# Small tasks of a mixing stage placed behind chosen chunks of the next products, with a stated order, and the rotary tables moved into that stage

## The chip, the cores and the metric

The kernel runs on one core of a Trainium2 chip, as one program. The metric is the device time of one execution in microseconds (us). Besides the timed runs there is one profiled execution, whose trace records every instruction on the engines PE (matrix products), DVE (vector), ACT (scalar functions), POOL and on SP, which here issues most of the loads.

## The reference, cut to what matters

One decoder layer on 256 tokens of width 2048, in float32:

```
x1 = x + 1/2 * SwiGLU_1(RMSNorm(x))                 # "ffn1", d_ff = 5632
P  = RMSNorm(x1) @ w_in                             # one projection, cut into named pieces
     A: gated linear attention (GLA), 4 heads, per-token decay from a low-rank projection
     B: NSA, 8 query heads on 2 key/value heads: compressed + sliding-window branches, rotary, gates
     C: attention of 4 heads into 256 memory tokens (keys and values are mem @ wmem)
x2 = x1 + concat(A, B, C) @ w_out                   # A to C and this are the "mixing stage"
x3 = x2 + 1/2 * SwiGLU_2(RMSNorm(x2))               # "ffn2"
y  = RMSNorm(x3)
```

Rotary embedding turns queries and keys by angles position x inverse frequency; their sines and cosines are the "rotary tables".

## The kernel before, in words

**A product.** All 256 tokens are two blocks t of 128 rows, and the activations stay on chip. Each product runs over the weights in chunks: one load of 128x1024 values (two slices kk of 128 x 512; `chunk`, L299), issued by SP, into a buffer of the pool `raw`. `split` (L290, L291) makes of a chunk a rounded part h on ACT and the rest l = r - h on DVE. PE then multiplies three times for each (kk, t), h by the activations' h (L304), l by their h (L305), h by their l (L306; `mm3`): 12 matmuls of 128x512 a chunk, 8 chunks for a product of 512 columns (agq has 296 columns, and chunks of 128x592).

**Slabs.** The two feed-forward stages go by slabs of 512 hidden columns. A slab is computed either in a form with seven products of half size, or "plain". By count of the built program the first takes 174 product matmuls and the second 192. `ffn(..., plain=(1,))` makes slab 1 of ffn1 plain. Each slab begins by turning activations (transposes of `c` or `g`, L390), which marks its place in the trace.

**Small tasks.** Everything else is small: transposes, norms, softmaxes, decay factors, score products. The framework schedules them among the product's instructions for each engine, and puts in the semaphore waits. The engines then work through their orders without exchanging any. A pool's buffer is free again when the readers of what lay there are done. Pools of a new stage are laid over those of the stage before in the order in which the dictionaries `FFN_SB`, `MIX_SB` list them.

**Places that matter here.** `prepare` computes the rotary tables on DVE in steps during ffn1's slab 1: nine pieces, each L616, L610, L611, L612, L618 (see `frac` and the loop over `PIECES`), then the tables ckn, skn, cqn, sqn (L631 to L633). At the end of ffn1 `last_of_ffn1` turns the last 512 columns of the residual `acc` (L341) and finishes the sums of squares. The mixing stage runs the projections agq, gkks (then kc), gv, gr, kwvs, vw and the queries; after gkks the keys of the first set are normed and turned through the rotary tables (`ra`, L772 to L776) and transposed (L786). GLA's decay levels (L827, L849) and masked products stand between gkks and gv. `nsa_group(g, ...)` runs eight steps of scores (L1028 to L1030), softmax, transposes of the weights `e` (L1072) and their product with values (L1077); at the end of a block come L1103 and L1108. `mem_heads` norms the memory queries and keys and transposes them (L1131). wmem is multiplied (two products), memory attention (L1156) follows, then wout, whose evictions add to `acc` (L1203), and ffn2, whose first chunk again needs the last 512 columns turned (L341).

Of the kernel before, what the change touches and what calls it, by code (L numbers as in the profile page):

```python
# [188 lines left out]
def _body(tc, A):  # L189
# [10 lines left out]
    def stage(name, sb, ps):  # L200

        stages.close()
        P.clear()
        sizes.clear()
        for n, b in ps.items():
            P[n] = stages.enter_context(tc.tile_pool(name=name + n, bufs=b, space=PSUM, reuse_waits="tile"))
        for n, (b, size) in sb.items():
            P[n] = stages.enter_context(tc.tile_pool(name=name + n, bufs=b, reuse_waits="tile"))
            sizes[n] = size
# [74 lines left out]

    def split(r, parts=1):
        n = r.shape[1]
        h, l = hi(n), lo(n)
        for i in range(parts):
            sl = slice(i * n // parts, (i + 1) * n // parts)
            act.activation(h[:, sl], r[:, sl], AF.Copy)  # L290
            dve.tensor_sub(l[:, sl], r[:, sl], f(h[:, sl]))  # L291
        return h, l

# [9 lines left out]
    def mm3(out, ah, al, wh, wl, first, last):  # L303
        pe.matmul(out, ah, wh, start=first, stop=False)  # L304
        pe.matmul(out, ah, wl, start=False, stop=False)  # L305
        pe.matmul(out, al, wh, start=False, stop=last)  # L306

    def mmchunk(banks, ah, al, k0, w, first, last):
        h, l = w
        n = h.shape[2]  # L310
        for kk, t in ((0, 0), (1, 0), (0, 1), (1, 1)) if first else ((0, 0), (0, 1), (1, 0), (1, 1)):
            sl = slice(t * 128, t * 128 + 128)
            mm3(banks[t][:, :n], ah[:, k0 + kk, sl], al[:, k0 + kk, sl], h[:, kk], l[:, kk],
                first and kk == 0, last and kk == 1)
# [20 lines left out]
    def transposed(j, g, th, tl):  # L335
        for k in range(4):
            if k % 2 == 0:
                pt = tbank().rearrange("p (k t) -> p k t", k=2)
# [249 lines left out]
    def prepare():  # L588

        early = raw(N_EARLY)  # L590
        nc.sync.dma_start(early, A["early"])
        C.update({n: early[:, o:o + w] for n, (o, w) in EARLY.items()})
        nc.sync.dma_start(kept, A["kept"])
        posi = sbuf("raw", "posi", I32, 3)
        nc.sync.dma_start(posi, A["pos"])
        posf = small(3, "posf")
        dve.tensor_copy(posf, posi)
        rots = raw(), raw()
# [36 lines left out]


        dve.tensor_copy(identb, ident)
        for i in range(2):
            dve.tensor_copy(maskb[:, i], C["tri"])
        r = raw(1024)  # L640
        nc.sync.dma_start(r, A["lmask"])
        dve.tensor_copy(lmask.rearrange("p l t -> p (l t)"), r)
# [25 lines left out]
    def before1(at):  # L668
# [12 lines left out]
        elif at[0] == 1:  # L681
            next(prep, None)
        elif at == (3, 10):
            norm_mem()

    prep = prepare()
    ffn("ffn1", hh, hl, r1, after1, before1, plain=(1,))
    xh, xl = st1["h"], st1["l"]
    r2, rm, r2q, r2n = (keep.tile([128, 2], F32, name=n) for n in ("r2", "rm", "r2q", "r2n"))

    def last_of_ffn1(c):
        if c == 1:
            norm_and_turn1(3)
            dve.tensor_copy(r2, finish_ss(ss1))
            dve.tensor_copy(rm, finish_ss(ssm))
            dve.tensor_scalar_mul(r2q, r2, 0.125)
            dve.tensor_scalar_mul(r2n, r2, -1.0)
# [5 lines left out]

    def scaled(dst, src, s):
# [4 lines left out]
    own = stages.enter_context(tc.tile_pool(name="own", bufs=1))  # L709
# [4 lines left out]
    for dst, sl in ((lev.rearrange("p l t -> p (l t)"), slice(0, 1024)), (levb, slice(1024, 1152))):  # L714
        r = raw(sl.stop - sl.start)
        nc.sync.dma_start(r, A["lev"][:, sl])
        act.activation(dst, r, AF.Copy)
    b = proj("agq", last_of_ffn1)
    ga = own.tile([128, 2, 17], F32, name="ga")
    dve.memset(ga, 1.0)  # L720
    gates = own.tile([128, 2, 24], F32, name="gates")
# [10 lines left out]
    pt = tbank()  # L732
    for t in range(2):
        pe.transpose(pt[:17, t * 128:t * 128 + 128], ga[:, t], ident)
    act.activation(gaT[:17], pt[:17, :256], AF.Copy)
    la = []
    xs, ex = (t512(n).rearrange("p (t d) -> p t d", t=2) for n in ("xs", "ex"))
    for t in range(2):
        pa = mbank()[:, :256]
        pe.matmul(pa, gaT[:17, t * 128:t * 128 + 128], C["wab"][:17], start=True, stop=True)  # L740
        act.activation(xs[:, t], pa, AF.Copy)
    dve.scalar_tensor_tensor(ex, xs, -1.0, xs, op0=ALU.mult, op1=ALU.min)
    act.activation(ex, ex, AF.Exp)
    act.activation(ex, ex, AF.Ln, bias=1.0)
    dve.scalar_tensor_tensor(xs, xs, 0.0, ex, op0=ALU.min, op1=ALU.subtract)
    for t in range(2):
        lah, lal = part(lab, t, 256), lab[:, t * 512 + 256:t * 512 + 512]
        act.activation(lah, xs[:, t], AF.Copy)
        dve.tensor_sub(lal, xs[:, t], f(lah))
        la.append((lah, lal))  # L750

    b = proj("gkks")
# [65 lines left out]
    for t in range(2):  # L818
        pool.memset(at[t], 0.0)
        for hp in range(2):  # L820
            hsl = slice(hp * 128, hp * 128 + 128)
            tsl = slice(t * 128, t * 128 + 128)
            dec = part(sb, 3 + 2 * hp, 1024).rearrange("p (l t) -> p l t", l=8)
            for half in range(2):
                pb = mbank()
                tm = lev[:, 4 * half:4 * half + 4].rearrange("p l t -> p (l t)")
                pe.matmul(pb, la[t][0][:, hsl], tm, start=True, stop=False)  # L827
                pe.matmul(pb, la[t][1][:, hsl], tm, start=False, stop=t == 0 or half == 0)
                if t == 1 and half == 1:
                    pe.matmul(pb[:, 384:], la[t][0][:, hsl], levb, start=False, stop=False)  # L830
                    pe.matmul(pb[:, 384:], la[t][1][:, hsl], levb, start=False, stop=True)
                act.activation(dec[:, 4 * half:4 * half + 4], pb.rearrange("p (l t) -> p l t", l=4), AF.Exp)
            for pl, s in enumerate(SIZES):
                for odd in range(2):
                    dv = dec[:, pl].rearrange("p (b o s) -> p b o s", o=2, s=s)[:, :, odd]
                    sv = gT[:, 1 - odd, hp, tsl].rearrange("p (b o s) -> p b o s", o=2, s=s)[:, :, odd]
                    dve.tensor_tensor(dv, dv, sv, op=ALU.mult)
            dve.tensor_tensor(far[:, hp, t], dec[:, 7], gT[:, 1 - t, hp, tsl], op=ALU.mult)
            for i0 in range(0, 8, 4):
                pbs = [mbank().rearrange("p (l t) -> p l t", l=4) for h in range(2)]  # L840
                for li in range(4):
                    i = i0 + li
                    for h in range(2):
                        ps = slice(64 * h, 64 * h + 64)
                        if i == 7:
                            lhs, rhs = gT[ps, 1, hp, tsl], gT[ps, 0, hp, tsl]
                        else:
                            lhs = rhs = dec[ps, i]
                        pe.matmul(pbs[h][:, li], lhs, rhs, start=True, stop=True)  # L849
                for h in range(2):  # L850
                    for li in range(4):
                        dve.copy_predicated(at[t][:, 2 * hp + h], lmask[:, i0 + li], pbs[h][:, li])
    pbs = [mbank() for h in range(2)]
    for hp in range(2):
        for h in range(2):
            ps = slice(64 * h, 64 * h + 64)
            pe.matmul(pbs[h][:, hp * 128:hp * 128 + 128], far[ps, hp, 0], far[ps, hp, 1], start=True, stop=True)
    for h in range(2):
        act.activation(at[2].rearrange("p (a b) t -> p a b t", b=2)[:, :, h],
                       pbs[h][:, :256].rearrange("p (a t) -> p a t", a=2), AF.Copy)  # L860
# [66 lines left out]
    b = proj("gv", spread("k", 0))  # L927
# [5 lines left out]
    b = proj("gr", spread("k", 4))  # L933
# [12 lines left out]
    for t in range(2):  # L946
# [13 lines left out]
    oh, ol = t16("oh"), t16("ol")  # L960
# [6 lines left out]
    for t in range(2):  # L967
# [9 lines left out]
    b = proj("kwvs", spread("v", 0))  # L977
# [26 lines left out]
    def pipelined(n, scores, softmax, apply):  # L1004
        scores(0)
        softmax(0)
        for i in range(n):
# [3 lines left out]
            if i + 1 < n:  # L1011
                softmax(i + 1)

    def nsa_group(g, qT):
# [96 lines left out]
        pipelined(8, scores, softmax, apply)  # L1111
# [9 lines left out]
    def mem_heads(b, rr, g, dst):  # L1121
        for t in range(2):
# [6 lines left out]
            pt = tbank().rearrange("p (h t) -> p h t", h=4)  # L1129
            for h in range(4):  # L1130
                pe.transpose(pt[:, h], v3[:, h], ident)  # L1131
            act.activation(dst[:, :, t * 128:t * 128 + 128], pt, AF.Copy)

    b = proj("mq")
    mem_heads(b, r2, C["mqn"], mT[0])
    nsa_group(1, q1)
    for i in range(2):
        b = [bank(), bank()]
        for c in range(4):
# [6 lines left out]
            for e in range(2):  # L1146
                mmchunk(b, h, l, 2 * e, chunk(A["wmem"][i, 2 * c + e]), c == e == 0, c == 3 and e == 1)
        if i == 0:
            mT.append(b4("mT").rearrange("p (h t) -> p h t", h=4))
            mem_heads(b, rm, C["mkn"], mT[1])  # L1150
# [112 lines left out]
```

## Time and the profile before

| | |
|---|---|
| median of 3 runs | 1850.74 us (1849.97 to 1850.81) |
| the profiled execution's own time | 1849.49 us |
| its span in the trace | 1847.7 us |
| PE busy in the span | 1824.6 us (99%), 8483 matmuls |
| DVE busy | 1618.7 us (88%) |
| ACT busy | 1076.6 us (58%) |

The span runs from the first to the last recorded instruction; some 1.8 us of the execution's time lie around it. Busy time counts an engine's records and overlaps within a pipelined engine are merged. A matmul's record of 0.39 us is longer than the pitch from one to the next, since they are pipelined, so the pitch is what a matmul costs.

### The profile page before, as it was taken

What the parts mean: (1) busy time and instruction counts of PE and PEld (TensorE: products, weight loads), DVE (VectorE), ACT (ScalarE), POOL (GpSimd) and SP (SyncE); (2) the same over time, 40 slices, a digit from 0 to 9 for tenths busy, and PEclk for the clock granted to TensorE, in tenths of its full rate; (3) what the DMA queues carried; (4) which work ended last, traced back from release to release, by engine and by line L of the source; (5) the groups of instructions that cost most, each with busy time, mean ns of one, the idle gap of its engine ahead of it and who ended that gap; (6) DMA issues with size and microseconds to landing.
All of it is one profiled execution on the core that took longest, in us unless ns stands there. A gap on an engine that the chain in (4) does not pass through costs nothing.

```text
span 1847.7 us, 23758 instructions
## 1 busy us (share of the span) xinstructions
PE 1824.6 (99%) x8483; PEld 1486.1 (80%) x8483; DVE 1618.7 (88%) x2075; ACT 1076.6 (58%) x1366; POOL 81.1 (4%) x106
## 2 busy tenths in 40 slices
PE   8999999999999999999999999999999999999997
PEld 6888888888888888777877787888888888888886
DVE  8989999999999986667677854999999999999996
ACT  7455665566556557533457643656656565665564
POOL 0000000000000000001000000000000000000000
PEclk9999999999999999999999999999999999999999
DMA  9677877677767735555644554776778677766771
GB/s 347 232 231 239 297 213 219 230 246 218 228 229 234 222 134 198 167 183 169 231 147 137 171 183 147 260 254 198 234 232 255 197 224 240 253 206 217 239 236 72
DMA packets 111224, 395.78 MB, mean 214 GB/s; under 512 B 12544, under 2 KB 12800, under 8 KB 110976
## 3 DMA queue, kind: packets, MB, share of 16 engines
q1 hardware_dynamic: 102896, 364.36, 56.7%
q0 software_dynamic: 8208, 29.89, 9.2%
q8 instruction: 67, 1.10, 0.2%
q14 instruction: 53, 0.43, 0.1%
HBM read 392.10 MB, written 2.10 MB: 213 GB/s over the span
## 4 chain that ended last, share of the span: by engine, by line
PE 92%; DVE 4%; DMA 1%; ACT 1%; issue 1%; POOL 1%; SPq 0%; ACTq 0%; POOLq 0%; DVEq 0%
PE pm L305 21%; PE pm L304 21%; PE pm L306 21%; PE px L304 8%; PE px L306 8%; PE px L305 8%; PE pt L390 1%; DVE l L291 1%; DMA r<-ffn1g 1%; PE pm L884 1%; POOL y L328 0%; PE px L849 0%; PE pt L341 0%; DVE exg L940 0%; PE po L1077 0%
## 5 line engine op out<-in xcount | busy, mean ns | idle before, releaser
L290 ACT ACTIVATE h<-r 128x1024 fp32r<-128x1024 f32 (+2 forms) x829 | 869.9, 1052 | 641.0 <-PE pm L306 477.7
L291 DVE TENSOR_TENSOR l<-r,h 128x1024 fp32r<-128x1024 f32 (+2 forms) x829 | 981.2, 1207 | 128.1 <-ACT h L290 115.9
L304 PE MATMUL px<-h,gx 128*128 128x512 f32 x616 | 239.9, 389 | 0.0
L306 PE MATMUL px<-h,gx 128*128 128x512 f32 x616 | 239.9, 389 | 0.0
L305 PE MATMUL px<-l,gx 128*128 128x512 f32 x616 | 239.9, 389 | 0.0
L304 PE MATMUL pm<-h,sh 128*128 128x512 f32 x456 | 179.7, 394 | 0.0
L305 PE MATMUL pm<-l,sh 128*128 128x512 f32 x456 | 179.3, 393 | 0.0
L306 PE MATMUL pm<-h,sl 128*128 128x512 f32 x456 | 178.0, 390 | 0.0
L305 PE MATMUL pm<-l,hh 128*128 128x512 f32 x398 | 155.5, 391 | 2.6 <-DVE l L291 2.6
L304 PE MATMUL pm<-h,hh 128*128 128x512 f32 x398 | 154.2, 391 | 0.8 <-ACT h L290 0.8
L306 PE MATMUL pm<-h,hl 128*128 128x512 f32 x398 | 154.9, 390 | 0.0
L305 PE MATMUL pm<-l,zh 128*128 128x512 f32 x364 | 142.7, 392 | 0.3 <-DVE l L291 0.3
L306 PE MATMUL pm<-h,zl 128*128 128x512 f32 x364 | 142.6, 392 | 0.0
L304 PE MATMUL pm<-h,zh 128*128 128x512 f32 x364 | 142.1, 391 | 0.0
L304 PEld LDWEIGHTS px<-h,gx 128*128 128x128 f32 x616 | 115.7, 188 | 24.1 <-issue 0.2
L305 PEld LDWEIGHTS px<-l,gx 128*128 128x128 f32 x616 | 115.7, 188 | 23.9
L306 PEld LDWEIGHTS px<-h,gx 128*128 128x128 f32 x616 | 115.7, 188 | 23.9
L305 PE MATMUL pm<-l,xh 128*128 128x512 f32 (+2 forms) x320 | 120.2, 376 | 1.1 <-DVE l L291 1.0
L304 PE MATMUL pm<-h,xh 128*128 128x512 f32 (+2 forms) x320 | 121.3, 380 | 0.0
L306 PE MATMUL pm<-h,xl 128*128 128x512 f32 (+2 forms) x320 | 120.4, 377 | 0.0
L404 DVE SCALAR_TENSOR_TENSOR acc<-px,acc 128x512 f32<-128x512 f32 x154 | 105.6, 686 | 6.3 <-PE px L306 4.6
L306 PEld LDWEIGHTS pm<-h,sl 128*128 128x128 f32 x456 | 85.7, 188 | 17.5
(336 smaller groups left out, 2630.7 us busy)
## 6 DMA issues: line engine op xcount, KB each, us to landing
r<-ffn1u SPq DMA_DIRECT2D x88, 512.0 KB, 5.0
r<-ffn1d SPq DMA_DIRECT2D x88, 512.0 KB, 4.8
r<-ffn2u SPq DMA_DIRECT2D x88, 512.0 KB, 4.8
r<-ffn2d SPq DMA_DIRECT2D x88, 512.0 KB, 4.8
r<-ffn1g SPq DMA_DIRECT2D x87, 512.0 KB, 5.1
r<-ffn2g SPq DMA_DIRECT2D x87, 512.0 KB, 5.1
r<-wout SPq DMA_DIRECT2D x32, 512.0 KB, 3.3
r<-ffn2u POOLq DMA_DIRECT2D x30, 512.0 KB, 7.4
```

The source lines that it names most:

```text
L290: act.activation(h[:, sl], r[:, sl], AF.Copy)
L291: dve.tensor_sub(l[:, sl], r[:, sl], f(h[:, sl]))
L304: pe.matmul(out, ah, wh, start=first, stop=False)
L305: pe.matmul(out, ah, wl, start=False, stop=False)
L306: pe.matmul(out, al, wh, start=False, stop=last)
L390: pe.transpose(pt[:, k], g[:, k * 128:k * 128 + 128], ident)
L404: dve.scalar_tensor_tensor(a, pd, 0.5, a, op0=ALU.mult, op1=ALU.add)
L884: pe.matmul(pcs[n][32 * p:32 * p + 32], flats[n][:, c * 4 + p], r[:, p * 256:p * 256 + 256], start=c == 0, stop=c == 7, tile_position=(0, ...
```

## The change

Eight things change.

- `prepare` becomes `rotary`, a sequence of steps in the mixing stage: it makes one step at each chunk of agq and of gkks, and what is left follows gkks. Its table `early` (128x704) and `posi` are loaded into the mixing stage's pools `b4` and `ev`. Constants that `prepare` also loaded are made at one point of ffn1 (`constants`).
- ffn1 has no plain slab any more.
- The pools are listed in another order, so that in the mixing stage `b4` lies over ffn1's `hi`, and `wk`, `ev` and `own` over its `lo`, with `raw`, `hi` and `lo` behind them.
- At ffn1's end and at the end of the mixing stage the last transposes go in two parts behind the splits and products of chunks 1 and 2 of the next product, squares behind chunk 4, the sums behind chunk 5, and copies behind chunk 7.
- `behind_products` states that an instruction stands, on its engine, behind the last product instruction (or split) written so far.
- GLA's steps are called at chunks of gv and gr, and its output and its transposes at chunks of kwvs.
- The transposes of the memory heads come at the second half of the next memory product's first load.
- Memory attention goes by one step at each half chunk of the second memory product, and at chunks 1 to 5 of wout's first product.

```diff
-FFN_SB = {"raw": (11, 1024), "hi": (6, 1024), "lo": (6, 1024), "gx": (1, 2048), "wk": (5, 512)}
-MIX_SB = {"raw": (6, 1024), "hi": (5, 1024), "lo": (5, 1024), "b4": (6, 1024), "wk": (6, 512), "ev": (2, 512)}
+FFN_SB = {"hi": (6, 1024), "lo": (6, 1024), "raw": (11, 1024), "gx": (1, 2048), "wk": (5, 512)}
+MIX_SB = {"b4": (6, 1024), "wk": (6, 512), "ev": (2, 512), "own": None, "raw": (6, 1024), "hi": (5, 1024),
+          "lo": (5, 1024)}
...
-MIX_PS = {"pm": 3, "px": 2, "pt": 2, "po": 1}
+MIX_PS = {"px": 2, "pt": 2, "po": 1, "pm": 3}
...
+    def behind_products(*engines):
+
+        ex = ExitStack()
+        for i in [done[e] for e in engines or done]:
+            ex.enter_context(tc.issue_after(getattr(i, "ins", i)))
+        return ex
...
-    def prepare():
-
-        early = raw(N_EARLY)
+    def rotary():
+
+        early = b4("early")[:, :N_EARLY]
         nc.sync.dma_start(early, A["early"])
         C.update({n: early[:, o:o + w] for n, (o, w) in EARLY.items()})
-        nc.sync.dma_start(kept, A["kept"])
-        posi = sbuf("raw", "posi", I32, 3)
+        posi = sbuf("ev", "posi", I32, 3)
         nc.sync.dma_start(posi, A["pos"])
         posf = small(3, "posf")
+        yield
         dve.tensor_copy(posf, posi)
...
-    ffn("ffn1", hh, hl, r1, after1, before1, plain=(1,))
+    ffn("ffn1", hh, hl, r1, after1, before1)
...
+    def turn_last(c, ss, g, th, tl):
+
+        if c in (1, 2):
+            with behind_products():
+                transposed(3, g, th, tl, range(2 * c - 2, 2 * c))
+        if c == 4:
+            with behind_products():
+                square_acc(ss, 3)
...
+    rot = rotary()
+
+    def first_of_mix(c):
+        last_of_ffn1(c)
+        next(rot, None)
+        if c == 5:
+            load_levels()
...
-    b = proj("gkks")
+    b = proj("gkks", both(lambda c: next(rot, None), placed((1, turn_ga), (3, log_decay))))
+    for _ in rot:
+        pass
...
-    b = proj("gv", spread("k", 0))
+    lv, dc = (lambda i: lambda: levels(*divmod(i, 2))), (lambda i: lambda: decayed(*divmod(i, 2)))
+    b = proj("gv", both(spread("k", 0), placed((1, lv(0)), (3, lv(1)), (4, dc(0)), (5, lv(2)), (6, dc(1)),
+                                               (7, lv(3)))))
...
-    b = proj("gr", spread("k", 4))
+    b = proj("gr", both(spread("k", 4), placed((1, dc(2)), (3, dc(3)), (4, far_products))))
...
-    b = proj("kwvs", spread("v", 0))
+    b = proj("kwvs", both(spread("v", 0), placed((1, lambda: gla_out(0)), (2, lambda: gla_out(1)),
+                                                 (4, lambda: turn_out(0)), (5, lambda: turn_out(1)))))
...
+                if (c, e) == (1, 0):
+                    with behind_products("pe"):
+                        turn_mem()
                 mmchunk(b, h, l, 2 * e, chunk(A["wmem"][i, 2 * c + e]), c == e == 0, c == 3 and e == 1)
+                if i == 1 and c > 0:
+                    with behind_products("pe"):
+                        next(mem_attention, None)
...
     def before2(at):
-        if at == 1:
-            norm_and_turn2(3)
-            dve.tensor_copy(r3, finish_ss(ss2))
+        if at in range(8):
+            turn_last(at, ss2, C["g2"], zh, zl)
```

Three places in the engines' orders show what these lines do. First the queue of SP at the end of ffn1, where the last loads of ffn1 (ffn1d) are followed by the first loads of the mixing stage (win_agq); `[waits ...]` lists the semaphores by which a load is held. Before:

```order
L299 DMA r<-ffn1d 128x1024 [waits DMAHW6_49,DVE_49]
L716 DMA r<-lev 128x1024 [waits DMAHW2_49,DMAHW7_49,DVE_49,Activation_49]
L716 DMA r<-lev 128x128 [waits DMAHW6_49,DMAHW0_49,DVE_49]
L299 DMA r<-win_agq 128x592 [waits DMAHW4_49,DMAHW1_49]
L299 DMA r<-win_agq 128x592
L299 DMA r<-win_agq 128x592 [waits DMAHW3_49]
```

Of the change:

```order
L309 DMA r<-ffn1d 128x1024 [waits DMAHW4_49,DVE_49]
L611 DMA posi<-pos 128x3 [waits DMAHW5_49,DVE_49,PE_49]
L608 DMA early<-early 128x704 [waits DMAHW6_49,Activation_49]
L309 DMA r<-win_agq 128x592 [waits DMAHW7_49,DMAHW0_49]
L309 DMA r<-win_agq 128x592
L309 DMA r<-win_agq 128x592 [waits DMAHW1_49]
```

Two loads have moved ahead of all of agq, and the first of them waits for PE. The semaphore's value is that of the last matmul but one of ffn1, which reads the last buffer of ffn1's pool `lo`, over which `posi` is laid.

The second place is DVE at the same point: the last eviction of ffn1 into `acc` (L404 before, L414 in the change), then the splits of agq (l<-r,h 128x592; L291, now L294). Before:

```order
L404 SCALAR_TENSOR_TENSOR acc<-pm,acc 128x512
L291 TENSOR_TENSOR l<-r,h 128x592 x2
L333 SCALAR_TENSOR_TENSOR xl<-pt,gains,xh 128x256
L351 TENSOR_REDUCE s_6110<-ss_127 128x2
L291 TENSOR_TENSOR l<-r,h 128x592
```

Of the change:

```order
L414 SCALAR_TENSOR_TENSOR acc<-pm,acc 128x512
L625 MEMSET rot 128x192
L614 CAST posf<-posi 128x3
L616 CAST maskb<-early 128x128 x2
L621 TENSOR_TENSOR rot<-early,posf 128x192
L623 CAST rot<-rot 128x192
L624 TENSOR_TENSOR rot<-rot 128x192
L635 TENSOR_SCALAR rot<-rot 128x192
L629 TENSOR_SCALAR rot<-rot 128x192
L294 TENSOR_TENSOR l<-r,h 128x592
L630 TENSOR_SCALAR rot<-rot 128x192
L294 TENSOR_TENSOR l<-r,h 128x592
```

The first split of agq now stands behind ten rows of the rotary tables, and the later splits alternate with the pieces (L635, L629, L630, L631, L637 in the new numbering).

The third place is PE at the end of the second NSA group, from its last scores (px<-kT,qT) on; `mh` are the memory keys' heads, and the product matmuls around it are those of wmem (L304 to L306 before, L314 to L316 in the change). Before, the last steps stand so:

```order
L1072 MATMUL pt<-ident,e 128x128 x4
L306 MATMUL pm<-h,l 128x512
L304 MATMUL pm<-h 128x512
L305 MATMUL pm<-l,h 128x512
L306 MATMUL pm<-h,l 128x512
L304 MATMUL pm<-h 128x512
L305 MATMUL pm<-l,h 128x512
L1077 MATMUL po<-pT,vsw 128x128 x4
L306 MATMUL pm<-h,l 128x512
L1103 MATMUL pt<-ident,scm 16x128 x4
L304 MATMUL pm<-h 128x512
L305 MATMUL pm<-l,h 128x512
```

Of the change, from the last scores to the next product:

```order
L1104 MATMUL px<-kT_6478,qT 128x272
L1105 MATMUL px<-kT_6478,qT 128x256
L1106 LDWEIGHTS identb
L1106 MATMUL px<-maskb,identb 128x256
L1148 MATMUL pt<-ident,e 128x128 x4
L1153 MATMUL po<-pT,vsw 128x128 x4
L1148 MATMUL pt<-ident,e 128x128 x4
L1179 MATMUL pt<-ident,scm 16x128
L1153 MATMUL po<-pT,vsw 128x128 x4
L1179 MATMUL pt<-ident,scm 16x128 x3
L1214 MATMUL pt<-ident,mh 128x128 x4
L1184 MATMUL po<-pcT,vcmp 128x128 x4
```

No product stands between the last steps any more. By count, 52 product matmuls stood from the sixth step's scores to the group's end, and 12 stand there now; the other 40 stand behind.

## Rows read from the trace of the kernel before

**Rows 1.** The page's part 1: busy time, share of the span, instructions of each engine.

```profile
PE 1824.6 (99%) x8483; PEld 1486.1 (80%) x8483; DVE 1618.7 (88%) x2075; ACT 1076.6 (58%) x1366; POOL 81.1 (4%) x106
```

**Rows 2.** Windows: stretch, length, busy us of PE, PEld, DVE, ACT, POOL, clock, DMA.

```profile
300.00:700.00 400.00, 400.00 (x1797) 330.28 (x1796) 381.47 (x399) 243.51 (x260) 13.81 (x16) 1.00 0.67 213
700.00:1145.00 445.00, 438.07 (x2304) 343.79 (x2302) 294.90 (x639) 231.29 (x456) 27.39 (x36) 1.00 0.51 170
...
752.00:840.00 88.00, 86.58 (x513) 64.86 (x512) 54.28 (x156) 36.41 (x49) 0.00 (x0) 1.00 0.57 185
```

**Rows 3.** Timeline of PE: transposes that open slab 1 and slab 2, ffn1 then ffn2.

```profile
59.39 0.60 PE L390 MATMUL pt<-ident,g 128*128 128x128 f32 x4
...
124.31 0.60 PE L390 MATMUL pt<-ident,c 128*128 128x128 f32 x4
...
1197.50 0.60 PE L390 MATMUL pt<-ident,g 128*128 128x128 f32 x4
...
1259.65 0.60 PE L390 MATMUL pt<-ident,c 128*128 128x128 f32 x4
```

**Rows 4.** Groups by line, DVE, 50 to 130 us: first and last of 17 rotary groups.

```profile
L612 DVE TENSOR_TENSOR r<-r 128x192 f32<-128x192 f32 x11 | 3.9, 357 | 0.3
...
L597 DVE CAST posf<-posi 128x3 f32<-128x3 int32 x1 | 0.2, 158 | 0.0
```

**Rows 5.** Windows: the stretch from ffn1's end to the first key transposes.

```profile
706.00:754.00 48.00, 46.73 (x252) 39.65 (x252) 34.05 (x56) 31.49 (x53) 5.73 (x10) 1.00 0.68 230
```

**Rows 6.** Timeline of DVE, then PE: last eviction, first split and product, first key transposes.

```profile
706.38 0.68 DVE L404 SCALAR_TENSOR_TENSOR acc<-pm,acc 128x512 f32<-128x512 f32 x1
706.97 1.45 DVE L291 TENSOR_TENSOR l<-r,h 128x592 fp32r<-128x592 f32 x2
...
706.71 0.52 PE L304 MATMUL pm<-h,xh 128*128 128x296 f32 x2
...
748.74 0.44 PE L786 MATMUL pt<-ident,ra 128*128 128x128 f32 x2
```

**Rows 7.** DMA issues, 686 to 716 us: KB, median us to landing; waits of SP, 640 to 716.

```profile
r<-win_agq SPq DMA_DIRECT2D x8, 296.0 KB, 3.9
...
SPq L716 <- DVE l L291: 25.3, 2, 15.6
```

**Rows 8.** Timeline of PE: the second NSA group's last steps, then the memory keys' transposes.

```profile
1012.78 0.72 PE L1028 MATMUL px<-kT,qT 128*128 128x272 f32 x2
...
1015.52 0.60 PE L1072 MATMUL pt<-ident,e 128*128 128x128 f32 x4
...
1024.69 0.63 PE L1072 MATMUL pt<-ident,e 128*128 128x128 f32 x4
...
1026.54 1.05 PE L1077 MATMUL po<-pT,vsw 128*128 128x128 f32 x8
...
1027.74 0.60 PE L1103 MATMUL pt<-ident,scm 128*16 128x128 f32 x4
...
1029.20 1.15 PE L1108 MATMUL po<-pcT,vcmp 16*128 16x128 f32 x8
...
1035.32 0.63 PE L1131 MATMUL pt<-ident,mh 128*128 128x128 f32 x4 [0.86 <-DVE mh L1128]
```

**Rows 9.** Timeline of DVE, then PE, from the end of wout into ffn2.

```profile
1143.49 1.37 DVE L1203 TENSOR_TENSOR acc<-pm,acc 128x512 f32<-128x512 f32 x2 [10.55 <-PE pm L306]
...
1146.98 0.69 DVE L291 TENSOR_TENSOR l<-r,h 128x512 fp32r<-128x512 f32 x1
...
1143.74 0.39 PE L306 MATMUL pm<-h,ol 128*128 128x512 f32 x1
...
1146.74 0.71 PE L304 MATMUL pm<-h,zh 128*128 128x512 f32 x2
...
1151.84 0.70 PE L304 MATMUL pm<-h,zh 128*128 128x512 f32 x2
```

**Rows 10.** Windows: two us of the same stretch.

```profile
1148.00:1150.00 2.00, 2.00 (x6) 1.54 (x6) 1.75 (x3) 0.96 (x2) 0.00 (x0) 0.50 1.01 404
```

More of the change, by code (lines that the diff above doesn't have):

```diff
@@ L282, in _body @@
         pe.matmul(pw, warm[:, :128], warm, start=i == 0, stop=i == WARM - 1)
+    done = {}
     def split(r, parts=1):
@@ L305, in mm3 @@
         pe.matmul(out, ah, wl, start=False, stop=False)
-        pe.matmul(out, al, wh, start=False, stop=last)
+        return pe.matmul(out, al, wh, start=False, stop=last)
     def mmchunk(banks, ah, al, k0, w, first, last):
@@ L702, in proj, with placed, before, both @@
         return b
+    def placed(*tasks):
+        tasks = dict(tasks)
+        def before(c):
+            if c in tasks:
+                with behind_products("pe"):
+                    tasks[c]()
+        return before
+    def both(*hooks):
+        def before(c):
+            for h in hooks:
+                h(c)
+        return before
     def scaled(dst, src, s):
@@ L817, in _body @@
     SIZES = [64, 32, 16, 8, 4, 2, 1]
-    for t in range(2):
-        pool.memset(at[t], 0.0)
-        for hp in range(2):
[L821 to L852, printed above, removed]
@@ new lines, in decayed @@
+    def decayed(t, hp):
+        dec = decs[t, hp]
+        tsl = slice(t * 128, t * 128 + 128)
+        for i0 in range(0, 8, 4):
+            pbs = [mbank().rearrange("p (l t) -> p l t", l=4) for h in range(2)]
+            for li in range(4):
+                i = i0 + li
+                for h in range(2):
+                    ps = slice(64 * h, 64 * h + 64)
+                    if i == 7:
+                        lhs, rhs = gT[ps, 1, hp, tsl], gT[ps, 0, hp, tsl]
+                    else:
+                        lhs = rhs = dec[ps, i]
+                    pe.matmul(pbs[h][:, li], lhs, rhs, start=True, stop=True)
+            for h in range(2):
+                for li in range(4):
+                    dve.copy_predicated(at[t][:, 2 * hp + h], lmask[:, i0 + li], pbs[h][:, li])
@@ L945, in _body, with gla_out @@
     ovs = []
-    for t in range(2):
+    def gla_out(t):
         pb = mbank()
@@ L1182, in _body, with mem_out @@
                 scaled(mv[:, t], b[t], rm[:, t:t + 1])
-    for h in range(4):
+    def mem_out(h):
         po = mbank()[:, :256]
@@ L1188, in _body, with mem_end @@
         dve.tensor_sub(ol[:, 12 + h], po, f(oh[:, 12 + h]))
+    def mem_end(c):
+        if 1 <= c <= 4:
+            with behind_products("pe"):
+                next(mem_attention, None)
+        if c == 5:
+            for _ in mem_attention:
+                pass
+            with behind_products("pe"):
+                for h in range(4):
+                    mem_out(h)
     ss2 = keep.tile([128, 2, 4], F32, name="ss2")
@@ L1199, in _body @@
         pd = [bank(), bank()]
-        product(pd, oh, ol, A["wout"][j])
+        product(pd, oh, ol, A["wout"][j], mem_end if j == 0 else None)
         for t in range(2):
```

183 lines of the change are left out of this document (116 added, 67 removed).

## The prediction, made before the changed kernel ran

> **What bounds the kernel now.** I read the page's engine totals first [rows 1]: PE is busy 99% of the span, DVE 88%. A gain can therefore only come from fewer matmuls, from less PE idle time, or from a better granted clock. The windows say where each lies [rows 2]. From 300 to 700 us, inside ffn1, PE never idles: 1797 products in 400.00 us, so one product matmul costs 0.2226 us. DVE is busy 381.47 of those 400, so there is little room beside PE in a feed-forward stage. From 700 to 1145 us, the mixing stage, PE is idle 445.00 - 438.07 = 6.93 us and DVE has 150 us free. The other loss is at the end of the mixing stage, read from the timeline [rows 9]. After the last product of wout (its record begins at 1143.74) the next undisturbed product begins at 1151.84. Twelve products and six transposes stand between them, some 3.2 us of work in 7.9 us: about 4.6 us are lost. Part of it is the clock, granted at 0.50 from 1148 to 1150 us [rows 10].
>
> So everything that better-placed small tasks could give back in the mixing stage is at most those 6.9 us, and at the passage to ffn2 at most 4.6.
>
> **The change, part by part.** The sum is made against the profiled execution, 1849.49 us (span 1847.7 and 1.8 around it). The median of the three runs is 1.25 us above it, and I add that at the end.
>
> *a) Slab 1 of ffn1 in the seven-product form.* It needs 174 product matmuls and not 192: 18 fewer at 0.2226 us [rows 2] are 4.0 us. The trace confirms it by another road: slab 1 of ffn1, plain, takes 124.31 - 59.39 = 64.92 us from its first transposes to the next slab's, and the same slab of ffn2, not plain, 1259.65 - 1197.50 = 62.15 us [rows 3]. That is 2.8 us less, and rotary work stood in the first. **-4.0**, between -4.0 and -2.8. `constants` at slab 2 adds two loads and two casts to DVE, which has 5% free there [rows 2]: nothing.
>
> *b) From ffn1 to the first key transposes.* Before, this passage is nearly free: the last eviction of ffn1 begins at 706.38, the first agq product at 706.71 and the first key transposes at 748.74 [rows 6], 42 us after ffn1's last product, with PE busy 46.73 of 48 [rows 5]. Two things change.
>
> First the loads. The order of SP has `posi` ahead of every load of agq, and `posi` waits for the last matmul but one of ffn1. SP works its queue in order: it stood 25.3 us at the loads of `lev` behind a split of DVE [rows 7], and nothing else went out of that queue meanwhile. So agq, whose first loads had landed before ffn1 ended (its first split begins at 706.97 [rows 6]), is only issued then. An agq load takes 3.9 us (median) from issue to landing [rows 7]. The split follows (0.7 us of DVE a chunk [rows 6]), and in the change ten rotary rows, some 2 us, stand ahead of it on DVE. PE stands for about 5 to 6 us. The Trainium skill says the same of the queue ("DMA: Bandwidth & Descriptors", section "Anatomy of one DMA"): a semaphore wait is taken on the issuing sequencer, ahead of dispatch, and the DMA engines themselves never wait. Its fixed 2.0 us plus bytes over 436 GB/s would give 2.7 us for such a load, as an estimate, and with it the stall would be 1.2 us shorter; the row's 3.9 us decides.
>
> Second DVE. The rotary rows, 17 groups from 3.9 us down to 0.2 [rows 4], add up to 21.9 us. In the 48 us of [rows 5] DVE is busy 34.05. Together that is 56 us, 8 more than there is, and all of it must be done before the key transposes, which need the tables. DVE also has little to do in the first 4 us, until `early` has landed, where it had splits before: 2 more. The passage grows by **+10** us. The lower bound is the wait for the loads alone, +4.5 (all rotary rows hidden); the upper one adds the whole 8 + 5.5 us, and 1 for the clock, below: +14.
>
> *c) GLA's levels and masked products at chunks of gv and gr.* From 752 to 840 us PE is idle only 88.00 - 86.58 = 1.42 us [rows 2], and the same instructions remain. **-1.5**, from -3 (if some alternations of product and small task vanish too) to +1.
>
> *d) GLA's output at chunks of kwvs, compression moved in the order.* It waits for the same reciprocals and norms, now behind a chunk's 12 products (2.7 us of cover). **0**, between -2 and +2.
>
> *e) The end of the second NSA group.* Before, products lie between all its steps. Forty of them now stand behind the group, 40 x 0.2226 = 8.9 us of cover taken away. What the bare chain takes is read from the trace [rows 8]: from the scores (1012.78) to the transposes of `e` (1015.52) 2.74 us, from such transposes (1024.69) to the product with the values (1026.54) 1.85, to L1103 1.20, to L1108 1.46, and 1.1 for itself: 8.3 us from the last scores on. PE's own work in that stretch is some 5.6 us (scores 1.0, two sets of transposes 0.7, two of L1077's 1.7, L1103 0.4, the heads' transposes 0.7, L1108 1.1). So at least 2.7 us are idle, and the two steps before, with 12 products in all, lose something too. Against this the wait of 0.86 us before the heads' transposes [rows 8] goes. I take **+5**, near the middle between +2 (2.7 less the 0.86) and +8 (all cover lost, less the same).
>
> *f) Memory attention at half chunks.* Each step has 12 products (2.7 us) behind it, where it had as many before; oh and ol of the last heads are needed by wout only from its later chunks. **0**, up to +1.
>
> *g) From the mixing stage to ffn2.* The first splits of ffn2 now only stand behind the two additions to `acc` (1.37 us), the transposes at chunks 1 and 2. From the end of wout to the first l: 1.37 + 0.69 [rows 9], less two h products that need no l (0.45): 1.6 us of wait, and 0.5 for the later transposes. Before it was 4.6, so **-2.5**, between -3.5 and -1.5. The clock had fallen to 0.50, the lower level, 1.2 GHz, after PE had waited most of the time from 1144 on; with the shorter wait I take it to stay at its upper level, 2.4 GHz.
>
> Sum: -4.0 + 10 - 1.5 + 0 + 5 + 0 - 2.5 = **+7.0 us**: 1856.5 for a profiled execution, **1857.7** beside the median.
>
> **The rivals.** A measurement of this kernel tells a difference from no change from about 0.2% on, 3.7 us.
>
> *The small tasks stay covered (the other side).* DVE has 150 us free in the mixing stage [rows 2], and the framework may have found orders in which the rotary rows and the last NSA steps wait for nothing. Then b is its lower end, +4.5 (the load, which can't be hidden), e is -0.9 (the old wait gone), and the sum -4.0 + 4.5 - 1.5 - 0.9 - 2.5 = -4.4: 1846.3. It speaks for it that DVE is at 71% in the stretch of [rows 5]; against it that 34.05 + 21.9 is more than 48 there. It decides by the first key transposes: if they come less than 47 us after ffn1's last product, this is the case.
>
> *The gains and losses cancel.* Here the mechanism of b holds, but the rotary pieces fill half of what they would otherwise push out (b +7), and the group's end costs its lower end (e +2): the sum is +1, 1851.7, the same. The tail of b can be absorbed: what follows the key transposes on PE has DVE slack, 54.28 of 88 [rows 2].
>
> *The clock falls as well.* At 0.50 [rows 10] a product takes 0.43 us, and the stretch after the wait for wout's sums cost 1.7 us that way. PE waits some 5 us in b and nearly 3 in e. In b the engine then waits for DVE anyway, so that a slower PE hardly costs; in e it costs the whole. Two falls make +3.4: 1861. The Trainium skill ("TensorE: Matmul & The Clock Gate", section "What's actually happening") has it that throttled is the default and activity releases it. By that rule both waits bring such a stretch. The trace so far shows one at one wait.
>
> *The stated order doesn't let products run on.* If the small tasks that stand behind a chunk's products still stop PE, the change at g brings nothing (0 in place of -2.5), and the passage at b meets the same: +10 in the sum and 1861 again.
>
> **How the numbers follow.** The forecast as worked out 0.50; clock or stopped products, also slower, 0.15; cancelling 0.20; covered 0.15. So faster 0.15, same 0.20, slower 0.65. The predicted time is that of the likeliest, 1857.7, whose own range, with b from +7 to +12 and e from +3 to +7, is 1853 to 1862. The range that is to hold 8 times in 10 takes in most of the other cases: 1847 to 1864.
>
> **What would show each step.** a: 62.1 us between the slab transposes, and 7512 products. b: the first agq load issued at ffn1's end, PE idle for 5 to 6 us there, and some 52 us from there to the first key transposes, with DVE busy throughout. e: over 2.7 us idle on PE behind the last scores of the second group, waiting for DVE or ACT. g: one wait of about 1.6 us for the first l and a clock of 1.00. It is wrong if SP issues agq ahead of `posi`'s wait, if DVE idles in b, or if PE goes through e without a gap.

## The result, and the profile after

The changed kernel takes **1861.16 us** (median of 6 runs, 1860.73 to 1861.43), the kernel before in the same comparison 1849.25 us (median of 6). The ratio is **1.0064, with a 95% interval of 1.0054 to 1.0074**: slower by 11.9 us. The prediction was 1857.7 us, +7.0, with a range of 1847 to 1864.

I follow the difference through the program by points that both traces have. Three of them are in the rows ahead of the prediction; the others, of the kernel before, are these: the last product matmul of ffn1 in PE's timeline, then two evictions in ACT's (the memory queries' heads, scaled by r, and the memory keys' heads, scaled by rm).

```profile
705.72 0.40 PE L306 MATMUL pm<-h,gl 128*128 128x512 f32 x1
...
968.86 0.69 ACT L705 ACTIVATE mh<-pm,r 128x512 f32<-128x512 f32 x1 [1.04 <-PE pm L306]
...
1010.12 0.69 ACT L705 ACTIVATE mh<-pm,rm 128x512 f32<-128x512 f32 x1 [1.04 <-PE pm L306]
```

Of the changed kernel, PE's timeline at the same points: slab transposes of ffn1 and ffn2 (they answer to [rows 3]), the last product of ffn1, the first of agq, the first key transposes ([rows 6]), and the last product of wout ([rows 9]).

```profile
58.29 0.60 PE L400 MATMUL pt<-ident,g 128*128 128x128 f32 x4
...
120.51 0.60 PE L400 MATMUL pt<-ident,c 128*128 128x128 f32 x4
...
702.40 0.39 PE L316 MATMUL pm<-h,gl 128*128 128x512 f32 x1
...
707.47 0.86 PE L314 MATMUL pm<-h,xh 128*128 128x296 f32 x2 [4.68 <-DVE rot L635]
...
753.19 0.44 PE L845 MATMUL pt<-ident,ra 128*128 128x128 f32 x2 [1.35 <-DVE ra L835]
...
1158.43 0.39 PE L316 MATMUL pm<-h,ol 128*128 128x512 f32 x1
...
1208.74 0.60 PE L400 MATMUL pt<-ident,g 128*128 128x128 f32 x4
```

| point | before | after | after - before |
|---|---|---|---|
| opening of slab 2 of ffn1 | 124.31 | 120.51 | -3.8 |
| last product of ffn1 | 705.72 | 702.40 | -3.3 |
| memory queries' heads evicted | 968.86 | 971.71 | +2.9 |
| last product of wout | 1143.74 | 1158.43 | +14.7 |
| opening of slab 1 of ffn2 | 1197.50 | 1208.74 | +11.2 |
| end of the span | 1847.7 | 1859.1 | +11.4 |

So 3.8 us are gained by the opening of slab 2, of which 3.3 are left at the end of ffn1; 6.2 are lost between that end and the memory queries, **11.8 lost from there to the end of wout**, and 3.5 gained on the way into ffn2. Four windows of the changed kernel (columns as in [rows 2]; the clock is the third number from the end) show what PE and its clock did at the places of loss and gain.

```profile
706.00:712.00 6.00, 4.37 (x16) 3.99 (x17) 5.37 (x16) 4.19 (x9) 0.00 (x0) 0.52 0.98 333
1026.00:1036.00 10.00, 7.75 (x44) 6.55 (x45) 4.18 (x18) 5.30 (x17) 0.00 (x0) 0.83 0.00 0
1040.00:1058.00 18.00, 15.74 (x68) 12.56 (x69) 15.04 (x32) 11.01 (x22) 1.34 (x2) 0.91 0.61 189
1158.00:1166.00 8.00, 7.07 (x32) 5.20 (x31) 6.15 (x8) 2.95 (x5) 0.00 (x0) 1.00 0.76 287
```

**The passage from ffn1.** The timeline of SP shows the loads that answer to [rows 7], and its waits from 690 to 716 us what held the first of them:

```profile
702.60 0.33 SPq L611 DMA_DIRECT2D posi<-pos  x1
703.01 0.38 SPq L608 DMA_DIRECT2D early<-early  x1
703.49 2.28 SPq L309 DMA_DIRECT2D r<-win_agq  x5
...
SPq L611 <- PE pm L316: 18.0, 1, 18.0
```

SP stands 18.0 us at `posi`, waiting for PE. `posi` is issued 0.2 us after the last product of ffn1 has begun, and agq behind it. PE then waits 4.68 us for the first agq product. The row names a rotary row of DVE as what ended the wait, but the product (h times xh) doesn't use that row; it only ended last, and experiment 3, which keeps the rotary rows, is rid of the wait. The first h of agq, on ACT, explains it:

```profile
706.72 0.70 ACT L293 ACTIVATE h<-r 128x592 fp32r<-128x592 f32 x1 [6.63 <-DMA r<-win_agq]
```

ACT had waited for the load, and its split ends at 707.42; PE starts at 707.47. The clock behind the wait is the lower one, granted at 0.52 from 706 to 712 us. The trace agrees here with the rule of the Trainium skill named in the prediction ("TensorE: Matmul & The Clock Gate", section "What's actually happening"). The prediction had only put 1 us of it into the upper bound of this term.

**The end of the second NSA group.** PE's timeline there, to be read against [rows 8], where products stand in every gap (the first line is the last matmul of the memory keys' product):

```profile
1009.67 0.39 PE L316 MATMUL pm<-h,l 128*128 128x512 f32 x1
...
1020.54 0.48 PE L316 MATMUL pm<-h,l 128*128 128x512 f32 x1
...
1024.53 0.70 PE L1148 MATMUL pt<-ident,e 128*128 128x128 f32 x4 [0.78 <-DVE e L1137]
1025.97 1.16 PE L1153 MATMUL po<-pT,vsw 128*128 128x128 f32 x8 [0.75 <-ACT pT L1150]
1028.74 0.63 PE L1148 MATMUL pt<-ident,e 128*128 128x128 f32 x4 [1.61 <-DVE e L1137]
...
1032.19 1.06 PE L1214 MATMUL pt<-ident,mh 128*128 128x128 f32 x4
...
1034.60 0.66 PE L1214 MATMUL pt<-ident,mh 128*128 128x128 f32 x4
1035.01 0.47 PE L314 MATMUL pm<-h 128*128 128x512 f32 x1
...
1040.43 0.63 PE L1214 MATMUL pt<-ident,mh 128*128 128x128 f32 x4 [1.05 <-DVE mh L1207]
...
1043.34 0.50 PE L315 MATMUL pm<-l,h 128*128 128x512 f32 x1 [1.83 <-DVE l L294]
```

Between the product matmul that begins at 1020.54 and the one at 1035.01 no other begins. The same stretch in ACT's timeline, with the evictions of the memory heads (L746) and the copies of their transposes (L1215):

```profile
971.71 0.69 ACT L746 ACTIVATE mh<-pm,r 128x512 f32<-128x512 f32 x1 [1.04 <-PE pm L316]
...
974.54 0.72 ACT L746 ACTIVATE mh<-pm,r 128x512 f32<-128x512 f32 x1
...
1033.29 0.60 ACT L1215 ACTIVATE mT<-pt 128x512 f32<-128x512 f32 x1 [0.27 <-PE pt L1214]
1033.78 0.68 ACT L746 ACTIVATE mh<-pm,rm 128x512 f32<-128x512 f32 x1
...
1035.30 0.60 ACT L1215 ACTIVATE mT<-pt 128x512 f32<-128x512 f32 x1
1035.79 0.68 ACT L746 ACTIVATE mh<-pm,rm 128x512 f32<-128x512 f32 x1
```

The reader is to see the pairs. The pool `ev` has two buffers. The memory queries' heads lie in both from 971 and 974 us on, and are only free when they are transposed, now at the group's end (1032.19 and 1034.60). The memory keys' heads, evicted at 1010 before, take the same buffers, and so come right behind each of these transposes. By count of the records the keys' product is complete at 1010.1 us (its 96th matmul is the line at 1009.67), 23.7 us before its first eviction begins. Until then it holds two of the three banks of `pm`. By the same count the next product of wmem gets no further than 18 matmuls, the last at 1020.54: it needs two banks, and one is free. No chunk is used up then, so SP stands too: its waits from 1015 to 1060 us have

```profile
SPq L309 <- DVE l L294: 29.5, 5, 25.4
```

and the load share from 1026 to 1036 is 0.00. No wait of PE or ACT for these loads shows when products run again. The 1.83 us above are for a split on DVE, and DVE's timeline has it behind the norm of the memory keys' heads, which had come late and itself waits for POOL:

```profile
1041.46 0.69 DVE L1206 TENSOR_TENSOR mh<-mh,y 128x512 f32<-128x512 f32 x1 [1.18 <-POOL y L338]
1042.07 1.22 DVE L294 TENSOR_TENSOR l<-r,h 128x1024 fp32r<-128x1024 f32 x1
```

In the source the queries' transposes stand behind the first loads of wmem, but also behind the whole of `nsa_group(1, ...)`, whose transposes use the same pool `pt`; in the trace they come behind its last ones (L1179). That the order in this pool is what put them so late wasn't tested.

**The passage to ffn2.** DVE's and PE's timelines, which answer to [rows 9]:

```profile
1158.17 1.37 DVE L1305 TENSOR_TENSOR acc<-pm,acc 128x512 f32<-128x512 f32 x2 [10.55 <-PE pm L316]
1159.46 2.42 DVE L294 TENSOR_TENSOR l<-r,h 128x512 fp32r<-128x512 f32 x3
...
1160.20 0.50 PE L315 MATMUL pm<-l,zh 128*128 128x512 f32 x1 [0.93 <-DVE l L294]
```

The splits come directly behind the two additions, one wait of 0.93 us is left, and the clock stays at 1.00.

### The profile page after: what moved, and what is told of

Same layout as the page of the kernel before. It is cut to its first block, busy times and chain, and to the rows that moved or that the text cites. A ratio compares the mean times of both kernels' runs of the same rounds, so it can differ in the third digit from the quotient of the medians.

```text
span 1859.1 us, 23765 instructions
## 1 busy us (share of the span) xinstructions
PE 1825.2 (98%) x8465; PEld 1485.9 (80%) x8465; DVE 1643.0 (88%) x2101; ACT 1088.6 (59%) x1377; POOL 86.4 (5%) x109
## 4 chain that ended last, share of the span: by engine, by line
PE 92%; DVE 3%; DMA 2%; ACT 1%; issue 1%; POOL 1%; SPq 0%; ACTq 0%; POOLq 0%; DVEq 0%
PE pm L314 20%; PE pm L315 20%; PE pm L316 20%; PE px L316 8%; PE px L315 8%; PE px L314 8%; PE pt L400 1%; DVE l L294 1%; DMA r<-ffn1g 1%; PE pm L951 1%; PE px L914 1%; PE po L1153 0%; DMA r<-ffn1u 0%; POOL y L338 0%; POOL y L337 0%
## 5 line engine op out<-in xcount | busy, mean ns | idle before, releaser
L293 ACT ACTIVATE h<-r 128x1024 fp32r<-128x1024 f32 (+1 forms) x838 | 878.9, 1052 | 643.9 <-PE pm L316 454.4
L294 DVE TENSOR_TENSOR l<-r,h 128x1024 fp32r<-128x1024 f32 (+1 forms) x838 | 992.2, 1210 | 102.6 <-ACT h L293 93.4
L316 PE MATMUL px<-h,gx 128*128 128x512 f32 x616 | 239.6, 389 | 0.0
L314 PE MATMUL px<-h,gx 128*128 128x512 f32 x616 | 239.6, 389 | 0.0
L314 PE MATMUL pm<-h,sh 128*128 128x512 f32 x480 | 188.9, 394 | 0.0
L315 PE MATMUL pm<-l,sh 128*128 128x512 f32 x480 | 188.4, 393 | 0.0
L316 PE MATMUL pm<-h,sl 128*128 128x512 f32 x480 | 187.3, 390 | 0.0
L315 PE MATMUL pm<-l,hh 128*128 128x512 f32 x364 | 142.0, 391 | 2.6 <-DVE l L294 2.6
L314 PE MATMUL pm<-h,zh 128*128 128x512 f32 x364 | 141.7, 390 | 0.0
L316 PE MATMUL pm<-h,zl 128*128 128x512 f32 x364 | 141.6, 389 | 0.0
L316 PE MATMUL pm<-h,hl 128*128 128x512 f32 x364 | 141.5, 389 | 0.0
L314 PE MATMUL pm<-h,hh 128*128 128x512 f32 x364 | 140.9, 391 | 0.6 <-ACT h L293 0.6
L314 PEld LDWEIGHTS px<-h,gx 128*128 128x128 f32 x616 | 115.6, 188 | 24.1
L316 PEld LDWEIGHTS px<-h,gx 128*128 128x128 f32 x616 | 115.6, 188 | 24.0
L314 PE MATMUL pm<-h,xh 128*128 128x512 f32 (+2 forms) x320 | 123.3, 386 | 5.4 <-DVE rot L635 4.7
L316 PE MATMUL pm<-h,xl 128*128 128x512 f32 (+2 forms) x320 | 121.4, 379 | 0.0
L414 DVE SCALAR_TENSOR_TENSOR acc<-px,acc 128x512 f32<-128x512 f32 x154 | 105.9, 688 | 6.6 <-PE px L316 5.4
L316 PEld LDWEIGHTS pm<-h,sl 128*128 128x128 f32 x480 | 90.2, 188 | 18.4
```

The lines of the kernel that those rows point to most:

```text
L293: done["act"] = act.activation(h[:, sl], r[:, sl], AF.Copy)
L294: done["dve"] = dve.tensor_sub(l[:, sl], r[:, sl], f(h[:, sl]))
L316: return pe.matmul(out, al, wh, start=False, stop=last)
L414: dve.scalar_tensor_tensor(a, pd, 0.5, a, op0=ALU.mult, op1=ALU.add)
```

## The experiments

Two theories stood after this: the loss at the memory products comes from the two held buffers of `ev`, and the loss behind ffn1 from the loads that stand behind `posi`. The rivals: small tasks at half chunks cost by themselves; DVE's rotary rows set the passage from ffn1. Each ratio is to runs of the kernel before in the same comparison (medians 1849.3 to 1849.6 us).

**1. The memory queries turned at once.**

```diff
-    turn_mem = mem_heads(b, r2, C["mqn"], mT[0])
+    mem_heads(b, r2, C["mqn"], mT[0])()
...
-                if (c, e) == (1, 0):
+                if i == 1 and (c, e) == (1, 0):
```

> One part undone: the memory queries' heads are transposed right behind their norm, as before the change; the memory keys' transposes stay placed. Theory (the heads that wait for their transposes hold both buffers of the pool ev, so the memory keys' product can't be evicted and wmem's second product has no bank): keys' eviction comes right behind their product, products stand again between the last steps of the second NSA group, and 9 to 11 of the 11.9 us come back: about 1851 us. Rival (the small tasks at half chunks, above all memory attention, cost by themselves): 1858 to 1861 us.

Measured: 1848.91 us, ratio 0.9998 (0.9988 to 1.0007). All of the loss comes back, 12.2 us. ACT's timeline has the keys' eviction right behind their product, and from 1020 to 1040 us PE is busy 19.11 of 20 us:

```profile
1013.13 0.69 ACT L746 ACTIVATE mh<-pm,rm 128x512 f32<-128x512 f32 x1 [1.04 <-PE pm L316]
...
1014.30 0.68 ACT L746 ACTIVATE mh<-pm,rm 128x512 f32<-128x512 f32 x1
...
1020.00:1040.00 20.00, 19.11 (x108) 15.07 (x108) 16.85 (x45) 14.41 (x38) 2.90 (x4) 1.00 0.47 159
```

**2. Four buffers in `ev`, the transposes left late.**

```diff
-MIX_SB = {"b4": (6, 1024), "wk": (6, 512), "ev": (2, 512), "own": None, "raw": (6, 1024), "hi": (5, 1024),
+MIX_SB = {"b4": (6, 1024), "wk": (6, 512), "ev": (4, 512), "own": None, "raw": (5, 1024), "hi": (5, 1024),
```

> The order of the source stays as in the change, the pool ev has 4 buffers instead of 2, and raw 5 instead of 6 to make room. Theory of the held buffers: the memory keys are evicted although the queries' transposes still come at the end of the group; 1851 to 1853 us, within 2 us of the kernel with the queries turned at once. Rival (it is where the transposes stand, not what they hold): no gain, 1859 to 1862 us.

Measured: 1846.42 us, ratio 0.9984 (0.9975 to 0.9993), 2.5 us better than experiment 1. The trace shows why it is more than expected: other pool sizes move `posi` too, so the wait behind ffn1 is gone as well (the first key transposes come at 750.25 us, 3 us earlier than in the changed kernel). For the question asked, the keys are evicted at once although the queries' transposes stay at the group's end:

```profile
1003.82 0.69 ACT L746 ACTIVATE mh<-pm,rm 128x512 f32<-128x512 f32 x1 [1.02 <-PE pm L316]
...
1028.15 0.60 PE L1214 MATMUL pt<-ident,mh 128*128 128x128 f32 x4
```

So it is what the late transposes hold, not where they stand. By the same product matmul counted in both traces, from the memory queries to the end of wout this kernel loses 1.7 us against the kernel before, where the change lost 11.8. (One buffer of `raw` was given up as well.)

**3. The positions in a tile of their own.**

```diff
-        posi = sbuf("ev", "posi", I32, 3)
+        posi = sm.tile([128, 3], I32, name="posi", tag="posi")
```

> Only the positions' tile moves out of the pool that lies over ffn1's buffers, so that no load waits for the last matmul but one of ffn1; all the rotary rows stay in the mixing stage. If the blocked loads set the loss at the passage from ffn1: the wait of 4.7 us before the first agq product and the half clock behind it go, 1855 to 1856 us. If DVE's rotary rows set it: the wait goes, but the key transposes still come 48 us or more after ffn1's last product, 1858 to 1861 us.

Measured: 1855.38 us, ratio 1.0033 (1.0022 to 1.0045): 5.8 us come back. SP now issues agq from 695.64 us on, 6.5 us before ffn1's last product; the wait at the first agq product is 0.88 us and not for a load:

```profile
703.43 0.51 PE L314 MATMUL pm<-h,xh 128*128 128x296 f32 x2 [0.88 <-DVE acc L414]
...
750.37 0.44 PE L845 MATMUL pt<-ident,ra 128*128 128x128 f32 x2 [0.75 <-DVE ra L835]
...
702.00:750.00 48.00, 45.57 (x237) 37.88 (x235) 45.85 (x126) 33.12 (x53) 5.07 (x9) 1.00 0.67 233
```

Half of the rival is right: DVE is busy 45.85 of these 48 us, and the key transposes still come 48 us behind ffn1's last product (702.17). But that lateness costs PE little: the passage is 5.2 us longer than before, and by count of the records 220 product matmuls lie in it, where before there were 206. The 14 more (3.1 us) had been put ahead of the key transposes by the framework.

**4. The rotary steps spread over ffn1**, two a slab (behind its steps 4 and 11), with three buffers of ffn1's `raw` held for them.

```diff
-        early = b4("early")[:, :N_EARLY]
+        early = raw(N_EARLY)
...
+        elif at[1] in (4, 11):
+            next(rot, None)
```

> The rotary steps go back into ffn1, two a slab over its slabs 1 to 9, with no plain slab, and their tables stay in three buffers of ffn1's raw. If DVE has room enough beside a slab in the seven-product form (5% of 62 us a slab, two steps of 1.7 us): the passage from ffn1 to the key transposes falls back to about 42 us, ffn1 grows by 0 to 3 us, 1854 to 1857 us. If DVE has none: each step stops PE for its length, 15 us or more are added in ffn1, 1868 us or more.

Measured: 1878.9 us, ratio 1.0163 (1.0146 to 1.018). ffn1 loses 23 us against the changed kernel (its last product begins at 725.78), as in the second case named. Whether by DVE's time or by the three buffers, this run alone doesn't say; the eighth does in part.

**5. Both repairs together** (experiments 1 and 3).

> The two repairs together: positions in a tile of their own, and the memory queries' heads transposed at once. If the two losses are separate, both gains add up: 1861.2 - 5.8 - 12.2 = 1843 us, about 6 us (0.3%) under the kernel before. If the two hang on one resource (the same pools' layout), less: 1847 to 1849 us.

Measured: **1843.71 us, ratio 0.9967 (0.9954 to 0.9979)**: the two losses add up (17.5 us come back, of 5.8 + 12.2), and this version beats the kernel before and the change.

**6. The kernel before with the new passage to ffn2 alone.** Its edit is `turn_last` and the new `before2` of the change's diff, put into the kernel before.

> The kernel before, with one part of the change alone: the last transposes, squares and sums in front of ffn2 placed behind chunks 1, 2, 4, 5 and 7. By the trace of the change this part gave 3.4 us: 1845.8 us, with a clock of 1.00 behind the last product of wout. If the gain came from the other order of the pools instead: 1849 us, no change.

Measured: 1846.37 us, ratio 0.9982 (0.9973 to 0.9991): 3.3 us, with the pools in their old order, and a clock of 1.00 from 1144 to 1152 us.

**7. Both repairs, memory attention as before the change.**

```diff
-                if i == 1 and c > 0:
-                    with behind_products("pe"):
-                        next(mem_attention, None)
...
-            mem_attention = pipelined(8, scores, softmax, apply)
+            turn_mem()
+            for _ in pipelined(8, scores, softmax, apply):
+                pass
```

> Both repairs, and memory attention again as before the change: its eight steps without a stated place, and the memory keys turned at once. If the steps at half chunks cost nothing by themselves, as forecast (0 to +1): within 1.5 us of the kernel with both repairs (about 1843). If they are what the second memory product loses: 3 us or more faster; if they help: 3 us or more slower.

Measured: 1844.02 us, ratio 0.9967 (0.9955 to 0.998), 0.3 us from experiment 5: the steps at half chunks neither cost nor bring anything that shows.

**8. Both repairs, eight buffers of `raw` in ffn1.**

```diff
-    stage("f1", FFN_SB, FFN_PS)
+    stage("f1", dict(FFN_SB, raw=(8, 1024)), FFN_PS)
```

> Both repairs, and ffn1's pool raw with 8 buffers instead of 11, which is what was left to the loads when the rotary tables were kept in three of them over ffn1. If the loss of the kernel with the rotary steps spread over ffn1 (23 us in ffn1) was the loads' missing buffers: ffn1 loses 15 to 23 us here as well, 1858 to 1866 us. If it was DVE's time: no loss, 1843 to 1845 us.

Measured: 1852.31 us, ratio 1.0012 (1.0003 to 1.0022): 8.6 us slower than experiment 5, between the two cases. In its profiled execution, the slowest of its runs, ffn1's last product comes 10.8 us later than in experiment 5's. So three missing buffers explain some 9 to 11 of the 23 us of experiment 4. The others lie in the rotary rows on DVE or in the two together; that wasn't separated.

**9. Both repairs, the rotary pieces computed twice.** The nine pieces run a second time, and the first sum is thrown away.

```diff
+        for again in range(2):
+            dve.memset(tot, 0.0)
...
-                yield
+                    if again or i % 2:
+                        yield
```

> Both repairs, and the nine rotary pieces computed twice (the first sum is thrown away): some 15 us more of DVE rows between ffn1 and the key transposes. If DVE's sum sets the passage, as the prediction had it: about 12 to 15 us slower than the kernel with both repairs (1843.7), 1856 to 1859 us. If PE is covered by products that the framework puts ahead of the key transposes: 0 to 5 us, 1844 to 1849 us.

Measured: 1846.39 us, ratio 0.9984 (0.9974 to 0.9993): by its trace 13.6 us more of DVE rows, which cost 2.7 us against experiment 5. The first key transposes now come at 774.10 us, 71.4 us behind ffn1's last product, where experiment 5 has 47.7. But by count of the records 317 product matmuls lie between the two points, where experiment 5 has 220: PE has products to do meanwhile.

**10. The kernel before with the held heads alone.** The memory queries are turned behind the first load of wmem, everything else as before.

```diff
-    mem_heads(b, r2, C["mqn"], mT[0])
+    turn_mem = mem_heads(b, r2, C["mqn"], mT[0])
...
+                if i == 0 and (c, e) == (1, 0):
+                    with behind_products("pe"):
+                        turn_mem()
```

> The kernel before, with one part of the change alone: the memory queries' heads are transposed behind the first load of wmem's first product, in place of at once. If the held buffers of ev are the cause of the loss at the second memory product: the 11.9 us appear here too, 1859 to 1862 us, with no product on PE in the last steps of the second NSA group. If the other parts of the change (pools' order, steps of memory attention at half chunks) are needed for it: 1849 to 1853 us.

Measured: 1859.81 us, ratio 1.0059 (1.0044 to 1.0074): this placing alone makes the kernel before 10.4 us slower. The window shows the same signs, a lower clock and no loads:

```profile
1020.00:1040.00 20.00, 16.55 (x73) 12.80 (x71) 9.35 (x31) 9.78 (x25) 3.05 (x4) 0.74 0.00 0
```

## Why the prediction was right in direction, and where its terms were off

- **a, slab 1** (-4.0): -3.8 at the opening of slab 2. Right. PE has 18 matmuls fewer in all (8465 for 8483). By count of the records 12 of these products are missing between the openings of slabs 1 and 2, which are 62.2 us apart as forecast, and 6 ahead of slab 1; so the forecast's "other road", 2.8 us, saw only a part. At the end of ffn1 0.5 us is gone again; no run shows why.
- **b, from ffn1 to the key transposes** (+10, between +4.5 and +14, whose terms add up to 14.5): 50.8 us after against 43.0 before (the 42 of the prediction are counted from the first agq product), less three more products (0.7): **+7.1**. The blocked loads are as described: issue at ffn1's end, 4.2 us (median) from issue to landing, so that the estimate of 2.7 beside the 3.9 of the row was too short, and 4.7 us of wait. They cost 5.8 us with the lower clock behind them (experiment 3), more than the 4.5 given. Nine rotary rows, not ten, stand ahead of the first split on DVE, and the first product, which needs only h, didn't wait for them. The step that was mis-sized is the second, "8 more than there is": the rotary rows cost about 2 us (5.2 less 3.1 in experiment 3). DVE is indeed the late engine, and the key transposes come 48 us after ffn1 even without the blocked loads. But a late task isn't a stopped PE: products put ahead of it fill the time, and experiment 9 shows that even 13.6 us more cost only 2.7.
- **c and d** (-1.5 and 0): together about -0.9, what is left of the 6.2 us between ffn1's end and the memory queries when b's 7.1 are taken off. That lies within what was given, but it is a remainder; no run measured these parts by themselves.
- **e, the end of the second group** (+5, between +2 and +8), **and f** (0 to +1): **+11.8 together**, outside both. Here the step failed that sized the loss by its cover: "all cover lost" was taken for the upper bound. The forty products that had moved behind the group were seen, but not asked what kept them there. It was the pool `ev` (experiments 1, 2 and 10); f has no part that shows (experiment 7). PE's waits between 1010 and 1060 us add up to 7.7 us (of DVE 5.8, of ACT 1.9), where 0.9 stood before. Of the rest the clock is the larger part. It was granted at 0.83 of 10 us and 0.91 of 18; with the lower level half the upper one, PE ran 3.4 and 3.2 us at 1.2 GHz, which, as an estimate, takes back about 3.3 us. Some 1.7 us are left that nothing here places. The upper bound had counted neither the clock nor the waits behind the late evictions (2.9 of the 7.7 us).
- **g, into ffn2** (-2.5): -3.5, at the edge of its range. The wait was 0.9 and not 1.6 us, and the clock stayed up as assumed.

The sum was right in sign and 4.9 us too small, with b 3 too high and e too low by 7. That it came as near as this is in part luck: the two errors have opposite signs, and the larger loss has a cause that the prediction didn't name.

Of the rivals, "the clock falls as well" took place at both waits that it named, as part of the two terms and not beside them; its 1861 is near the measured time, but it didn't have the held buffers either. "The stated order doesn't let products run on" didn't take place: g brought its gain. Nor did "stay covered", by its own sign: the key transposes came 50.8 us behind ffn1, over its limit of 47. Once the two lines are repaired the time falls below that rival's 1846.3 (experiment 5, 1843.7), but there the wait for the loads, which it kept, is gone, and the key transposes still come 47.7 us behind.

## What to carry to other kernels

When a task is moved back in the order, list what it holds while it waits: buffers of small pools above all, and who needs them next. Two buffers kept for 60 us held back the eviction of a product, with it two of PE's three banks, and then the splits and the loads. The Trainium skill has this as consistent bubbles that can mean too few buffers for the next tile ("Perfetto Trace Analysis", section "Optimization Strategy"); here the gap came once and did not repeat, and the rows that showed it were an eviction right behind an unrelated transpose.

A tile that is put into another pool inherits the waits of what lay there before, and in a queue that issues in order, as SP's did here, every load behind it inherits them too (agq behind `posi`: 4.68 us of wait on PE). And that an engine has more work than time does not price a delay: count the products that can go ahead of the late task.

## What the runs showed of the hardware that had not been expected

The clock's part was larger than forecast. It was granted at 0.52 from 706 to 712 us, and the 4.68 us wait had ended at 707.47. Experiment 3 took this wait down to 0.88 us, 3.8 us less, had a clock of 1.00 there, and gave back 5.8 us: more than the waiting that went. Behind the single wait of 0.93 us at ffn2 the clock stayed at 1.00.
